# The beginning of a two-layer decoder trunk written out: the first norm's weights on the transposed side, loads in turns, casts and low halves by k-tile

## The chip, the cores and the metric

One of the cores of a Trainium2 chip runs the whole program, one launch for both layers. The metric is the device time of one execution in microseconds (us), lower is better. The engines are called as in the profile: PE (TensorE, the matrix engine), PEld (its loads of stationary tiles), DVE (VectorE), ACT (ScalarE), POOL (GpSimd) and SP (SyncE, which here only issues DMAs).

## What is computed

The reference takes x of 256 x 1024 numbers in float32 and applies two layers, each of three sub-layers with a norm before and behind it:

```python
def rms_norm(x, g):
    y = x * lax.rsqrt(jnp.mean(x * x, axis=-1, keepdims=True) + EPS)
    return y * g

def swiglu(h, wi, wo):
    gate, up = jnp.split(h @ wi, 2, axis=-1)
    return (jax.nn.silu(gate) * up) @ wo

for l in range(2):
    x = x + 0.5 * rms_norm(swiglu(rms_norm(x, ffn1_pre_g[l]), ffn1_wi[l], ffn1_wo[l]), ffn1_post_g[l])
    x = x + rms_norm(hybrid_mixer(rms_norm(x, mix_pre_g[l]), ...), mix_post_g[l])
    x = x + 0.5 * rms_norm(swiglu(rms_norm(x, ffn2_pre_g[l]), ffn2_wi[l], ffn2_wo[l]), ffn2_post_g[l])
```

The change touches the very first rms_norm, of x with ffn1_pre_g[0], and the first two pieces of ffn1_wi[0], which is 1024 x 5632. The mixer (a gated, a windowed and a stick-breaking branch) is not touched.

## The kernel before

The 256 rows of x lie in two tiles of 128 rows, called tt = 0 and 1 (x0 and x1 in the trace). Products in float32 precision are made of three matmuls of a narrower type (fp32r): each operand is split into a high half (a cast) and a low half (what the cast left), and `mm3` (L391 to L395) adds high by high, low by high and high by low (L392, L393, L394).

**Weights.** The host packs all weights in 212 units of 1 MB, each 128 x 2048 numbers, in the order of use. `loader` (L161) brings a unit into one of two buffers called raw, by SP's queue, in an order kept by `load` (L113); `stream` lets the next unit go out when the buffer two back has been split. `splitter` (L213) casts each half unit to hi on ACT (L231) and subtracts it to lo on DVE (L232), into rings of eight halves. raw2 can thus be loaded only when the low halves of unit 0 are done, raw3 when those of unit 1 are, and so on by turns of two.

**Activations.** `prenorm` (L344) makes a norm: two Squares with their sums on ACT (L350), the power −1/2 on POOL (`rstd_of`, L315), the product xn of x, that factor rs and the weights gain on DVE (L360), then `to_T` (L335): per half, four transposes on PE into a tile tr (L339), and `hilo` (L330), which writes hh on ACT (L332) and hl on DVE (L333), each 128 x 512. The weights of a norm come by `gain` (L279) as a tile of 128 x 1024, a broadcast load of 512 KB.

**The first feed-forward.** A chunk (`chunk512`, L397) is 512 columns of wi, 256 of the gate and 256 of the other, for one row tile: 8 k-tiles, so 24 matmuls, over two units. Its product goes through Silu on ACT (L451) and a product on DVE (L452) into sg, and two transposes bring sg to gT, which the second matrix product (accumulators acc) uses. Four chunks with tt = 0 and 1 in turn come first; from the fifth on pairs of chunks are made with seven products instead of eight (`pair7`), which want sums of the activations: `sums` (L487) makes tiles sA on DVE (L491, L502, L506, L507, L513) and splits them (ACT L496, DVE L497). The quads of weights for this (wa, wb, wf) are in part loaded with accumulating DMAs.

**What sets the order.** The code is run by a model clock: each group of matmuls lets `ck` advance by the PE time it is given, and coroutines (the splitter, norms, sums, transposes of sg) say by `yield` how many us later they go on. So an instruction's place in its engine's row depends on this clock. Ahead of it all stands the beginning: x0, gain0, raw0 in two halves, x1 and raw1 are issued on SP one behind the other; `prenorm` of tt = 0 starts at 4.0, of tt = 1 at 10.0, the splitter at 7.0 of the model's time; ten warming matmuls of 128 x 128 on an identity run ahead on PE.

Of the kernel before, what the change touches and what calls it, by code (L numbers as in the profile page):

```python
# [9 lines left out]
F32 = mybir.dt.float32  # L10
# [64 lines left out]


@with_exitstack
def trunk(ctx, tc, x, wpk, gains, lnp, wst, bst, consts, out, depth=DEPTH):
    nc = tc.nc
    V, S, G, T = nc.vector, nc.scalar, nc.gpsimd, nc.tensor  # L80
    ck = Clock()
# [17 lines left out]
    def tr_tile(n):  # L99
        return ptr.tile([P, 512], F32, tag="tr", name=nm(n))  # L100
# [12 lines left out]
    def load(dst, src):  # L113

        i = nc.sync.dma_start(dst, src)
        if lastdma[0] is not None:
            tc.add_manual_dep(i.ins, lastdma[0].ins.name, NOSYNC, reason="load order")
        lastdma[0] = i
# [41 lines left out]

    def loader():  # L161

        ring = []

        def stream(key, u, first=False):
            while len(ring) >= 2 and ring[-2] not in done:
                yield
            ring.append(key)
            t = rp.tile([P, 2048], F32, tag="raw", name=f"raw{u}", bufs=2)
            raw[key] = [t[:, c] for c in WQ]  # L170
            for c in WQ if first else (slice(0, 2048),):
                load(t[:, c], wpk[u][:, c])

        def load_b(k):
            f = k.ffn
            i = "b" + str(k.par)
            if i not in f:
                f[i] = [sp.tile([P, 1024], F32, tag="q4", name=nm("wb"), bufs=9),
                        sp.tile([P, 1024], F32, tag="shl" if k.par else "q4", name=nm("wb"), bufs=1 if k.par else 9)]
            k.b = f[i]  # L180
            for q, c in enumerate(WQ):
                load(k.b[q], wpk[k.u12][:, c])
            for q, c in enumerate(WQ):
                nc.gpsimd.dma_start(k.b[q], wpk[k.u22][:, c], accum_op=ALU.add)

        for n, (kind, k) in enumerate(plan):
            if n + 4 < NI and plan[n + 4][0] == "B11" and not plan[n + 4][1].prev:
                load_b(plan[n + 4][1])
            if kind == "w":
                yield from stream(n, k, n == 0)  # L190
            elif kind == "B11":
                while k.prev and not k.prev.t1:
                    yield
                f = k.ffn
                if "a" not in f:
                    f["a"] = [sp.tile([P, 1024], F32, tag="q4", name=nm("wa"), bufs=9) for _ in WQ]
                raw[n] = f["a"]
                for q, c in enumerate(WQ):
                    load(f["a"][q], wpk[k.u11][:, c])
            elif kind in ("B21", "B22"):  # L200
                yield from stream(n, k.u21 if kind == "B21" else k.u22)
                if kind == "B21" and k.next:
                    load_b(k.next)
            yield
# [3 lines left out]
    def ready(n, kind, k):  # L208
        if kind[0] == "T":
            raw[n] = k.b if kind == "T3" else k.ffn["a" if kind == "T1" else "f"]  # L210
        return n in raw

    def splitter():  # L213
        for n, (kind, k) in enumerate(plan):
            while not ready(n, kind, k):
                next(ld)
            halves[n] = []
            for q in range(2):
                gate = place.get(n)
                while st_["free"] <= 0 if gate is None else not gate.on:  # L220
                    yield 0.2
                    gate = place.get(n)
                if gate is not None:
                    h = sp.tile([P, 1024], F32R, tag="q4", name=f"hi{n}_{q}", bufs=9)
                    lo = sp.tile([P, 1024], F32R, tag="q4", name=f"lo{n}_{q}", bufs=9)
                else:
                    st_["free"] -= 1
                    h = rp.tile([P, 1024], F32R, tag="hi", name=f"hi{n}_{q}", bufs=RING)
                    lo = rp.tile([P, 1024], F32R, tag="lo", name=f"lo{n}_{q}", bufs=RING)
                r = raw[n][q]  # L230
                S.copy(h, r)  # L231
                V.tensor_sub(lo, r, f32(h))  # L232
                halves[n].append((h, lo))
                yield 1.2
            if kind == "B11":
                f = k.ffn
                if "f" not in f:
                    f["f"] = [sp.tile([P, 1024], F32, tag="xn", name=nm("wf"), bufs=2) for _ in WQ]
                for q, c in enumerate(WQ):
                    V.tensor_add(f["f"][q], f["a"][q], k.b[q])  # L240
                    nc.gpsimd.dma_start(f["a"][q], wpk[k.u12][:, c], accum_op=ALU.add)
                    yield 0.6
            elif kind == "B21":
                for q in range(2):
                    V.tensor_add(k.ffn["f"][q], k.ffn["f"][q], raw[n][q])
                    yield 0.6
            elif kind == "T1":
                k.t1 = True
            done.add(n)
            for _ in range(3):  # L250
                next(ld, None)
# [31 lines left out]
            gl[i] = t  # L283
        return gl.get(i)

    load(xs[0], x[0:P, :])
    gain(0)
    next(ld)
    load(xs[1], x[P:SEQ, :])
    next(ld)  # L290

    mB_ = cp.tile([P, 1152], BF16, tag="mB", name="mB")
    mB = [mB_[:, 768:1152], mB_[:, 0:768]]
# [50 lines left out]
    def prenorm(tt, gi, flag, st=None):  # L344

        xn = sp.tile([P, DM], F32, tag="xn", name=nm("xn"), bufs=2)
        st = sp.tile([P, 2], F32, tag="ss", name=nm("ss"), bufs=4)
        for i, h in enumerate(HF):
            with tc.high_priority(offset=HOT):
                q = S.activation(xn[:, h], xs[tt][:, h], AF.Square, scale=DM ** -0.5, accum_out=st[:, i:i + 1])  # L350
                if gi == 0 and tt == 1:
                    tc.add_manual_dep(q.ins, lasthi[0].ins.name, NOSYNC, reason="first tile first")
            if i == 0:
                yield 0.6
        r = rstd_of(st[:, 0:1], st[:, 1:2])
        yield 1.7
        gn = gain(gi)
        with tc.high_priority(offset=HOT):
            for h in HF:
                V.scalar_tensor_tensor(xn[:, h], xs[tt][:, h], r, gn[:, h], op0=ALU.mult, op1=ALU.mult)  # L360
        yield 1.0
        for i, h in enumerate(HF):
            to_T(xn[:, h], tt, 4 * i, 4, hh, hl)
            yield 0.7
        flag.on = True

    def post_half(acc, yn, st, i, gi, mul):

# [555 lines left out]
            finish(tt, gi + 1, acc, us[3], hh, hl, 6, 6, KD, tt == 1, 1.0, nxt)  # L924


    ck.start(splitter(), 7.0)
    for tt in range(NT):
        hready[tt] = Flag()
        co = prenorm(tt, 0, hready[tt])  # L930
        ck.start(co, 4.0 + 6 * tt)
    warm = tr_tile("warm")
    for i in range(10):
        T.matmul(warm[:, 0:P], ident, ident, start=True, stop=True)
    for l in range(depth):
        b = 6 * l
        ffn(b, b + 2, l == 0)
# [101 lines left out]
```

## Time and profile before

| | us |
|---|---|
| median of 3 runs | 1259.87 |
| lowest and highest | 1258.27 and 1259.88 |
| the profiled execution | 1260.91 |
| its span in the trace | 1259.2 |
| PE busy | 1240.5 |
| DVE busy | 949.3 |
| ACT busy | 729.5 |
| POOL busy | 75.5 |

The profiled execution takes 1.7 us more than the span that the trace shows. Busy time says how long an engine executed; PE's busy time counts overlapping matmuls once. In a timeline a row is a run of like instructions: start, length from the first start to the last end, engine, line, operation, what it writes and reads, their count, and in brackets how long the engine stood idle before and what ended that. A row for two instructions is shorter than twice one, since the second begins before the first's end. In the chain of waits a DMA's row goes from issue to landing.

### The profile page before, as it was taken

The numbers are of one execution on the slowest core, as the hardware profiler recorded it, in microseconds if no ns is written. First come the engines' busy times: TensorE is split into PE (matmuls) and PEld (weight loads), VectorE is DVE, ScalarE is ACT, GpSimd is POOL, SyncE is SP. The second block draws the span as 40 slices with busy tenths as digits, with TensorE's granted clock in tenths as the row PEclk, the third lists the DMA queues.
The fourth block names the chain that finished last, engine by engine and source line by source line (L and its number), as shares of the span: only waits on it lengthen the run. The fifth ranks groups of instructions, "written<-read, shape, count | busy, mean of one in ns | idle before, by whom it ended". The sixth has DMA issues, their size and how long they took to land.

```text
span 1259.2 us, 16367 instructions
## 1 busy us (share of the span) xinstructions
PE 1240.5 (99%) x6284; PEld 1029.3 (82%) x6284; DVE 949.3 (75%) x1185; ACT 729.5 (58%) x996; POOL 75.5 (6%) x129
## 2 busy tenths in 40 slices
PE   8999999999999999999999999999999999999997
PEld 6777878998778878888878888789977788888886
DVE  5889977645765877899768899865467668689983
ACT  5566656435656465666645666654366655557652
POOL 0001001000000010010011010010000000110000
PEclk8999999999999999999999999999999999999999
DMA  7899555554435557885668785744543455687851
GB/s 251 279 316 264 172 201 194 188 212 166 136 134 178 192 167 271 261 270 167 239 207 260 252 258 185 236 175 161 210 181 119 149 173 200 213 240 250 250 195 65
DMA packets 45294, 259.41 MB, mean 206 GB/s; under 512 B 5280, under 2 KB 5408, under 8 KB 21280
## 3 DMA queue, kind: packets, MB, share of 16 engines
q1 hardware_dynamic: 38304, 233.20, 52.0%
q0 software_dynamic: 6912, 25.17, 10.5%
q8 instruction: 49, 0.80, 0.3%
q14 instruction: 29, 0.24, 0.1%
HBM read 257.30 MB, written 1.05 MB: 205 GB/s over the span
## 4 chain that ended last, share of the span: by engine, by line
PE 82%; DMA 6%; DVE 6%; ACT 3%; issue 1%; POOL 1%; SPq 0%; DVEq 0%; POOLq 0%; ACTq 0%
PE mm L392 15%; PE mm L394 15%; PE mm L393 15%; DMA raw<-wpk 5%; PE acc L394 5%; PE acc L393 5%; PE acc L392 5%; DVE lo L232 3%; PE qk L393 3%; PE qk L394 3%; PE qk L392 3%; PE tr L339 2%; ACT hi L231 2%; PE pj L394 1%; PE pj L392 1%; PE pj L393 1%
## 5 line engine op out<-in xcount | busy, mean ns | idle before, releaser
L232 DVE TENSOR_TENSOR lo<-raw,hi 128x1024 fp32r<-128x1024 f32 x376 | 451.8, 1220 | 153.2 <-ACT hi L231 148.1
L231 ACT CAST hi<-raw 128x1024 fp32r<-128x1024 f32 x376 | 387.2, 1050 | 259.4 <-DMA raw<-wpk 78.6
L392 PE MATMUL mm<-hi,hh 128*128 128x512 f32 x784 | 314.0, 401 | 1.7 <-ACT hh L332 1.7
L394 PE MATMUL mm<-hi,hl 128*128 128x512 f32 x784 | 307.3, 392 | 0.2 <-DVE hl L333 0.2
L393 PE MATMUL mm<-lo,hh 128*128 128x512 f32 x784 | 306.8, 391 | 0.0
L392 PEld LDWEIGHTS mm<-hi,hh 128*128 128x128 f32 x784 | 147.9, 189 | 33.3 <-issue 2.7
L394 PEld LDWEIGHTS mm<-hi,hl 128*128 128x128 f32 x784 | 147.7, 188 | 32.7 <-DVE hl L333 0.9
L393 PEld LDWEIGHTS mm<-lo,hh 128*128 128x128 f32 x784 | 148.1, 189 | 27.9
L392 PE MATMUL acc<-hi,gT 128*128 128x512 f32 x352 | 139.3, 396 | 0.2 <-ACT gT L332 0.2
L394 PE MATMUL acc<-hi,gT 128*128 128x512 f32 x352 | 137.6, 391 | 0.3 <-DVE gT L333 0.3
L393 PE MATMUL acc<-lo,gT 128*128 128x512 f32 x352 | 137.7, 391 | 0.0
L392 PE MATMUL qk<-hh,hi 128*128 128x256 f32 x320 | 91.2, 285 | 0.0
L394 PE MATMUL qk<-hh,lo 128*128 128x256 f32 x320 | 90.5, 283 | 0.0
L393 PE MATMUL qk<-hl,hi 128*128 128x256 f32 x320 | 90.5, 283 | 0.0
L392 PE MATMUL mm<-hi,sA 128*128 128x512 f32 x192 | 77.2, 402 | 0.8 <-DVE sg L479 0.8
L394 PEld LDWEIGHTS acc<-hi,gT 128*128 128x128 f32 x352 | 66.1, 188 | 14.3 <-DVE gT L333 0.8
L392 PEld LDWEIGHTS acc<-hi,gT 128*128 128x128 f32 x352 | 66.1, 188 | 13.5 <-ACT gT L332 0.7
L393 PEld LDWEIGHTS acc<-lo,gT 128*128 128x128 f32 x352 | 66.2, 188 | 13.0
L394 PE MATMUL mm<-hi,sA 128*128 128x512 f32 x192 | 75.1, 391 | 0.0
L393 PE MATMUL mm<-lo,sA 128*128 128x512 f32 x192 | 74.9, 390 | 0.0
L332 ACT CAST gT<-tr 128x256 fp32r<-128x256 f32 x88 | 32.5, 369 | 63.6 <-PE tr L339 63.5
L393 PEld LDWEIGHTS qk<-hl,hi 128*128 128x128 f32 x320 | 61.4, 192 | 0.1
(170 smaller groups left out, 1724.2 us busy)
## 6 DMA issues: line engine op xcount, KB each, us to landing
raw<-wpk SPq DMA_DIRECT2D x187, 1024.0 KB, 4.9
wb<-wpk SPq DMA_DIRECT2D x24, 512.0 KB, 7.0
wb<-wpk POOLq DMA_DIRECT2D x24, 512.0 KB, 9.2
wa<-wpk SPq DMA_DIRECT2D x24, 512.0 KB, 6.0
wa<-wpk POOLq DMA_DIRECT2D x24, 512.0 KB, 9.5
gain<-gains SPq DMA_DIRECT2D x12, 512.0 KB, 7.7
x<-x SPq DMA_DIRECT2D x2, 512.0 KB, 5.6
raw<-wpk SPq DMA_DIRECT2D x2, 512.0 KB, 6.5
```

Of the source, the lines that this page charges most:

```text
L231: S.copy(h, r)
L232: V.tensor_sub(lo, r, f32(h))
L332: lasthi[0] = S.copy(h_out, src)
L339: T.transpose(tr[:, k * P:(k + 1) * P], src[:, k * P:(k + 1) * P], ident)
L392: T.matmul(o, ah, bh, start=first, stop=False, skip_group_check=go_on)
L393: T.matmul(o, ah, bl, start=False, stop=False, skip_group_check=go_on)
L394: T.matmul(o, al, bh, start=False, stop=stop, skip_group_check=go_on)
```

## The change

The first norm and the first two units are no longer made by `prenorm`, `loader` and `splitter`, but by a new function `begin`, which says the order of ACT and of DVE row by row:

- The norm's weights come as gk, a tile of 128 x 8 (4 KB, one column per k-tile) by a DMA that ACT issues. The load of gain0 is gone. xn is x times rs alone, and the weights are applied behind the transposes: hh is an ACT activation (Copy) with a column of gk as scale, hl one DVE operation with that column, each per k-tile (128 x 128), so eight and eight for each row tile where there were two and two.
- x0 comes in two halves. The Square of its second half is on DVE.
- Loads go out in turns: x0, raw0's first half; raw0's second half behind the first Square; x1 behind the first cast; then raw1 in two halves. `loader` and `splitter` begin at unit 2.
- Unit 0 is cast by k-tile (128 x 512), and its low halves stand between the hl of the first group. x1's Squares stand behind the first cast of unit 1.
- Eleven warming matmuls run ahead, and two more between the two groups of transposes of x0.
- The splitter starts at 0.0 of the model's clock behind this, and the groups of tt = 1 are a coroutine `second` that starts with a wait of 3.0.

Its core; the tile sizes, the clock and all that follows the first feed-forward's code are as before:

```diff
@@ loader @@
-        ring = []
-
-        def stream(key, u, first=False):
+        ring = [0, 1]
...
-            for c in WQ if first else (slice(0, 2048),):
-                load(t[:, c], wpk[u][:, c])
+            load(t, wpk[u])
...
+            if n < 2:
+                continue
...
-    load(xs[0], x[0:P, :])
-    gain(0)
-    next(ld)
-    load(xs[1], x[P:SEQ, :])
-    next(ld)
...
-                if gi == 0 and tt == 1:
-                    tc.add_manual_dep(q.ins, lasthi[0].ins.name, NOSYNC, reason="first tile first")
...
+    gk = cp.tile([P, KD], F32, tag="gk", name="gk")
+    first = {}
+    def order(eng, i):
+        if eng in first:
+            tc.add_manual_dep(i.ins, first[eng].ins.name, NOSYNC, reason="order of the beginning")
+        first[eng] = i
+        return i
+    def scaled(tt, st):
+        xn = sp.tile([P, DM], F32, tag="xn", name=nm("xn"), bufs=2)
+        r = rstd_of(st[:, 0:1], st[:, 1:2])
+        for h in HF:
+            order("V", V.tensor_scalar(xn[:, h], xs[tt][:, h], r, None, op0=ALU.mult))
+        return xn
+    def group(xn, tt, i, lows):
+        tr = tr_tile("tr")
+        for k in range(4):
+            T.transpose(tr[:, k * P:(k + 1) * P], xn[:, (4 * i + k) * P:(4 * i + k + 1) * P], ident)
+        ck.pe(0.43)
+        for k in range(4):
+            kk = 4 * i + k
+            order("S", S.activation(hh[:, tt, kk, :], tr[:, k * P:(k + 1) * P], AF.Copy, scale=gk[:, kk:kk + 1]))
+        for k in range(4):
+            kk = 4 * i + k
+            lows[k]()
+            order("V", V.scalar_tensor_tensor(hl[:, tt, kk, :], tr[:, k * P:(k + 1) * P], gk[:, kk:kk + 1],
+                                              f32(hh[:, tt, kk, :]), op0=ALU.mult, op1=ALU.subtract))
+    def begin():
+        warm = sc_tile("warm")
+        def warmup(n):
+            for _ in range(n):
+                T.matmul(warm[:, 0:P], ident, ident, start=True, stop=True)
+        def after(i, j):
+            tc.add_manual_dep(i.ins, j.ins.name, mybir.DependencyInfo(
+                mybir.DependencyClass.Sync, mybir.DependencyReason.SCHED_ONLY), reason="loads in turn")
+        warmup(11)
+        nc.scalar.dma_start(gk, g0)
+        for h in HF:
+            load(xs[0][:, h], x[0:P, h])
+        rt = [rp.tile([P, 2048], F32, tag="raw", name=f"raw{u}", bufs=2) for u in range(2)]
+        ht, lt = [], []
+        for u in range(2):
+            for q in range(2):
+                ht.append(rp.tile([P, 1024], F32R, tag="hi", name=f"hi{u}_{q}", bufs=RING))
+                lt.append(rp.tile([P, 1024], F32R, tag="lo", name=f"lo{u}_{q}", bufs=RING))
+        st_["free"] -= 4
+        load(rt[0][:, WQ[0]], wpk[0][:, WQ[0]])
+        st = sp.tile([P, 2], F32, tag="ss", name=nm("ss"), bufs=4)
+        sq = sp.tile([P, DM], F32, tag="xn", name=nm("sq"), bufs=2)
+        i0 = order("S", S.activation(sq[:, HF[0]], xs[0][:, HF[0]], AF.Square, scale=DM ** -0.5,
+                                     accum_out=st[:, 0:1]))
+        order("V", V.scalar_tensor_tensor(sq[:, HF[1]], xs[0][:, HF[1]], 1.0 / DM, xs[0][:, HF[1]], op0=ALU.mult,
+                                          op1=ALU.mult, accum_out=st[:, 1:2]))
+        load(rt[0][:, WQ[1]], wpk[0][:, WQ[1]])
+        after(lastdma[0], i0)
+        def hi(n, k):
+            c = slice(512 * (k % 2), 512 * (k % 2) + 512)
+            return order("S", S.copy(ht[2 * n + k // 2][:, c], rt[n][:, 512 * k:512 * k + 512]))
+        def low(n, k):
+            c = slice(512 * (k % 2), 512 * (k % 2) + 512)
+            j = 2 * n + k // 2
+            order("V", V.tensor_sub(lt[j][:, c], rt[n][:, 512 * k:512 * k + 512], f32(ht[j][:, c])))
+        i1 = hi(0, 0)
+        hi(0, 1)
+        load(xs[1], x[P:SEQ, :])
+        after(lastdma[0], i1)
+        for q in range(2):
+            load(rt[1][:, WQ[q]], wpk[1][:, WQ[q]])
+        xn = scaled(0, st)
+        def lo2(k):
+            if k == 2:
+                hi(0, 2)
+                hi(0, 3)
+            low(0, k)
+        group(xn, 0, 0, [lambda k=k: lo2(k) for k in range(4)])
+        warmup(2)
+        group(xn, 0, 1, [lambda: None] * 4)
+        for q in range(2):
+            halves.setdefault(0, []).append((ht[q], lt[q]))
+        hready[0].on = True
+        for q in range(2):
+            j = 2 + q
+            order("S", S.copy(ht[j], rt[1][:, WQ[q]]))
+            if q == 0:
+                st = sp.tile([P, 2], F32, tag="ss", name=nm("ss"), bufs=4)
+                sq = sp.tile([P, DM], F32, tag="xn", name=nm("sq"), bufs=2)
+                for i, h in enumerate(HF):
+                    order("S", S.activation(sq[:, h], xs[1][:, h], AF.Square, scale=DM ** -0.5,
+                                            accum_out=st[:, i:i + 1]))
+            order("V", V.tensor_sub(lt[j], rt[1][:, WQ[q]], f32(ht[j])))
+            halves.setdefault(1, []).append((ht[j], lt[j]))
+            if q == 0:
+                xn = scaled(1, st)
+        for n in range(2):
+            done.add(n)
+            raw[n] = True
+        def second():
+            yield 3.0
+            for i in range(2):
+                group(xn, 1, i, [lambda: None] * 4)
+                yield 0.7
+            hready[1].on = True
+        ck.start(second(), 0.0)
...
-    ck.start(splitter(), 7.0)
     for tt in range(NT):
         hready[tt] = Flag()
-        co = prenorm(tt, 0, hready[tt])
-        ck.start(co, 4.0 + 6 * tt)
-    warm = tr_tile("warm")
-    for i in range(10):
-        T.matmul(warm[:, 0:P], ident, ident, start=True, stop=True)
+    begin()
+    ck.start(splitter(), 0.0)
...
+        "g0": np.ascontiguousarray(gains[0].reshape(KD, P).T),
```

On DVE, in the place of the first row tile's end and the second's beginning, the row before was this (xn, then low halves of unit 1, hl of tt = 1, low halves of units 2 and 3):

```order
L360 SCALAR_TENSOR_TENSOR xn_8_148<-x1_81,rs_10_159,gain0_83 128x512 x2
L232 TENSOR_TENSOR lo1_0_141<-raw1_89,hi1_0_140 128x1024
L232 TENSOR_TENSOR lo1_1_155<-raw1_89,hi1_1_154 128x1024
L333 TENSOR_TENSOR hl_95<-tr_11_189,hh_94 128x512
L333 TENSOR_TENSOR hl_95<-tr_13_206,hh_94 128x512
L232 TENSOR_TENSOR lo2_0_171<-raw2_138,hi2_0_170 128x1024
L232 TENSOR_TENSOR lo2_1_183<-raw2_138,hi2_1_182 128x1024
L452 TENSOR_TENSOR sg_14_213<-mm_7_144,sg_14_213 128x256
L232 TENSOR_TENSOR lo3_0_202<-raw3_168,hi3_0_201 128x1024
```

and it is now this, where gk is the small tile of weights:

```order
L468 TENSOR_TENSOR lo1_0_110<-raw1_104,hi1_0_109 128x1024
L378 TENSOR_SCALAR xn_10_170<-x1_81,rs_11_171 128x512 x2
L468 TENSOR_TENSOR lo1_1_112<-raw1_104,hi1_1_111 128x1024
L235 TENSOR_TENSOR lo2_0_185<-raw2_182,hi2_0_184 128x1024
L235 TENSOR_TENSOR lo2_1_195<-raw2_182,hi2_1_194 128x1024
L393 SCALAR_TENSOR_TENSOR hl_86<-tr_13_215,gk_87,hh_85 128x128 x4
L393 SCALAR_TENSOR_TENSOR hl_86<-tr_14_238,gk_87,hh_85 128x128 x4
L235 TENSOR_TENSOR lo3_0_209<-raw3_204,hi3_0_208 128x1024
L235 TENSOR_TENSOR lo3_1_232<-raw3_204,hi3_1_231 128x1024
```

The eight small hl of tt = 1 (L393) now stand behind the low halves of unit 2, and one low half of unit 1 stands ahead of xn.

On ACT, in the same place, the row before:

```order
L231 CAST hi1_0_140<-raw1_89 128x1024
L231 CAST hi1_1_154<-raw1_89 128x1024
L231 CAST hi2_0_170<-raw2_138 128x1024
L332 CAST hh_94<-tr_11_189 128x512
L332 CAST hh_94<-tr_13_206 128x512
L231 CAST hi2_1_182<-raw2_138 128x1024
L451 ACT_TABLE_LOAD
L451 ACTIVATE sg_14_213<-mm_7_144 128x256
```

and now:

```order
L461 CAST hi1_0_109<-raw1_104 128x1024
L466 ACTIVATE sq_9_166,ss_8_165<-x1_81 128x512 x2
L461 CAST hi1_1_111<-raw1_104 128x1024
L389 ACTIVATE hh_85<-tr_13_215,gk_87 128x128 x2
L234 CAST hi2_0_184<-raw2_182 128x1024
L234 CAST hi2_1_194<-raw2_182 128x1024
L389 ACTIVATE hh_85<-tr_13_215,gk_87 128x128 x2
L389 ACTIVATE hh_85<-tr_14_238,gk_87 128x128 x4
L569 ACT_TABLE_LOAD
```

x1's Squares stand between the two casts of unit 1, and six of the eight small hh behind both casts of unit 2.

On DVE again, from unit 7's low halves to the silu product sg that PE's transposes await, the row before:

```order
L232 TENSOR_TENSOR lo7_0_353<-raw7_289,hi7_0_352 128x1024
L232 TENSOR_TENSOR lo7_1_372<-raw7_289,hi7_1_371 128x1024
L507 TENSOR_TENSOR sA_34_394<-sA_30_369,sA_34_394 128x512
L491 TENSOR_TENSOR sA_41_446<-hh_94,hl_95 128x512
L513 TENSOR_TENSOR sA_41_446<-sA_41_446,sA_34_394 128x512
L232 TENSOR_TENSOR lo8_0_413<-raw8_350,hi8_0_412 128x1024
L232 TENSOR_TENSOR lo8_1_429<-raw8_350,hi8_1_428 128x1024
L497 TENSOR_TENSOR sA_33_391<-sA_30_369,sA_33_391 128x512
L497 TENSOR_TENSOR sA_38_421<-sA_34_394,sA_38_421 128x512
L497 TENSOR_TENSOR sA_40_443<-sA_29_367,sA_40_443 128x512
L497 TENSOR_TENSOR sA_42_461<-sA_41_446,sA_42_461 128x512
L452 TENSOR_TENSOR sg_45_469<-mm_39_424,sg_45_469 128x256
```

and now, where five more rows follow up to that product (four of the operation L615 that L497 was, then sg_47):

```order
L235 TENSOR_TENSOR lo7_0_388<-raw7_324,hi7_0_387 128x1024
L609 TENSOR_TENSOR sA_32_404<-hh_85,hl_86 128x512
L331 TENSOR_TENSOR gT_24_346<-tr_39_436,gT_24_346 128x256
L235 TENSOR_TENSOR lo7_1_407<-raw7_324,hi7_1_406 128x1024
L620 TENSOR_TENSOR sA_32_404<-sA_31_402,sA_32_404 128x512
L609 TENSOR_TENSOR sA_36_429<-hh_85,hl_86 128x512
L609 TENSOR_TENSOR sA_43_481<-hh_85,hl_86 128x512
L624 TENSOR_TENSOR sA_31_402<-sA_36_429,sA_31_402 128x512
L235 TENSOR_TENSOR lo8_0_448<-raw8_385,hi8_0_447 128x1024
L625 TENSOR_TENSOR sA_36_429<-sA_32_404,sA_36_429 128x512
L235 TENSOR_TENSOR lo8_1_464<-raw8_385,hi8_1_463 128x1024
L631 TENSOR_TENSOR sA_43_481<-sA_43_481,sA_36_429 128x512
```

Of the sums sA, two of the operation L609 (L491 before), one L620 (L502) and one L624 (L506), and one gT product, now stand behind the first low half of unit 7; they stood ahead of it.

On PE the transposes of that product were in this place before:

```order
L394 MATMUL mm_44_465<-hi6_1_340,hl_95 128x512
L392 MATMUL acc_26_359<-hi7_0_352,gT_22_311 128x512
L393 MATMUL acc_26_359<-lo7_0_353,gT_22_311 128x512
L339 MATMUL tr_46_488<-ident_73,sg_45_469 128x128 x2
L394 MATMUL acc_26_359<-hi7_0_352,gT_22_311 128x512
L392 MATMUL acc_27_360<-hi7_0_352,gT_22_311 128x512
```

and are now here:

```order
L512 MATMUL mm_46_500<-hi6_0_360,hl_86 128x512
L510 MATMUL mm_46_500<-hi6_1_375,hh_85 128x512
L511 MATMUL mm_46_500<-lo6_1_376,hh_85 128x512
L337 MATMUL tr_48_523<-ident_73,sg_47_504 128x128 x2
L512 MATMUL mm_46_500<-hi6_1_375,hl_86 128x512
L510 MATMUL mm_46_500<-hi6_1_375,hh_85 128x512
L511 MATMUL mm_46_500<-lo6_1_376,hh_85 128x512
L512 MATMUL mm_46_500<-hi6_1_375,hl_86 128x512
```

They stand six matmuls further forward: two of the accumulating ones (acc) were ahead of them, and now four of the last chunk's (mm) come behind them. In the rows of all engines past some 60 us, and of POOL from the start, names' numbers aside, before and after read alike.

## Rows read from the trace of the kernel before

**Rows 1.** The page's first part: engine, busy us, share of the span, instructions.

```profile
PE 1240.5 (99%) x6284; PEld 1029.3 (82%) x6284; DVE 949.3 (75%) x1185; ACT 729.5 (58%) x996; POOL 75.5 (6%) x129
```

**Rows 2.** Waits of PE over the span: us in total, times, longest.

```profile
PE tr L339 <- DVE sg L452: 3.0, 5, 1.5
...
PE mm L392 <- DVE sg L479: 0.8, 2, 0.6
```

**Rows 3.** Timeline of PE, 0 to 62 us.

```profile
7.62 1.38 PE L339 MATMUL tr<-ident,xn 128*128 128x128 f32 x8 [1.57 <-DVE xn L360]
10.66 0.79 PE L392 MATMUL mm<-hi,hh 128*128 128x512 f32 x1 [1.66 <-ACT hh L332]
...
20.71 0.39 PE L394 MATMUL mm<-hi,hl 128*128 128x512 f32 x1
...
56.16 0.44 PE L339 MATMUL tr<-ident,sg 128*128 128x128 f32 x2 [1.54 <-DVE sg L452]
```

**Rows 4.** Chain of waits, 0 to 62 us: start, length, what.

```profile
14.11 0.43 PE mm L392
...
20.42 0.23 PE mm L392
...
24.51 0.22 PE tr L339 x2
...
35.69 9.96 DMA raw<-wpk
```

**Rows 5.** Timeline of ACT, 0 to 62 us.

```profile
4.39 0.63 ACT L350 ACTIVATE xn<-x 128x512 f32<-128x512 f32 x1 [2.32 <-DMA x<-x]
...
5.54 0.19 ACT L350 ACTIVATION_READ_ACCUMULATOR xn<-x 128x1 f32 x1
...
19.87 1.28 ACT L451 ACT_TABLE_LOAD   x1
...
45.72 2.00 ACT L231 CAST hi<-raw 128x1024 fp32r<-128x1024 f32 x2 [4.12 <-DMA raw<-wpk]
```

**Rows 6.** Timeline of DVE, 0 to 62 us.

```profile
6.81 1.41 DVE L360 SCALAR_TENSOR_TENSOR xn<-x,rs,gain 128x512 f32<-128x512 f32 x2 [6.81 <-POOL rs L325]
8.88 2.50 DVE L232 TENSOR_TENSOR lo<-raw,hi 128x1024 fp32r<-128x1024 f32 x2 [0.66 <-ACT hi L231]
...
26.11 1.23 DVE L232 TENSOR_TENSOR lo<-raw,hi 128x1024 fp32r<-128x1024 f32 x1 [0.52 <-ACT hi L231]
...
38.37 1.28 DVE L491 TENSOR_TENSOR sA<-hh,hl 128x512 f32<-128x512 f32 x2
...
42.44 0.42 DVE L333 TENSOR_TENSOR gT<-tr,gT 128x256 fp32r<-128x256 f32 x1
...
46.80 2.36 DVE L232 TENSOR_TENSOR lo<-raw,hi 128x1024 fp32r<-128x1024 f32 x2 [3.35 <-ACT hi L231]
```

**Rows 7.** Windows: stretch, length, busy PE, PEld, DVE, ACT, POOL, PEclk, DMA, GB/s.

```profile
10.00:20.00 10.00, 9.18 (x31) 6.95 (x32) 7.77 (x11) 7.42 (x14) 0.88 (x2) 0.66 0.68 238
```

**Rows 8.** Groups of one form: busy us, mean ns, idle before, releaser.

```profile
L332 ACT CAST hh<-tr 128x512 fp32r<-128x512 f32 x32 | 18.6, 586 | 24.2 <-PE tr L339 24.1
...
L713 ACT ACTIVATE eC<-eC 128x768 f32<-128x768 f32 x16 | 13.5, 846 | 0.4
...
L713 ACT ACTIVATE pB<-pB,stB 128x768 f32<-128x768 f32 x8 | 7.5, 935 | 5.3 <-POOL stB L733 5.3
...
L656 DVE SCALAR_TENSOR_TENSOR u<-sv,bs,u 128x128 f32<-128x128 f32 x16 | 4.5, 343 | 0.0
...
L644 DVE TENSOR_SCALAR v<-v,bn,rs 128x512 f32<-128x512 f32 x4 | 2.2, 547 | 6.0 <-POOL rs L325 6.0
```

**Rows 9.** Loads of tile raw, 0 to 62 us.

```profile
DMA to landing us min/median/max: 4.8/6.1/10.0
```

**Rows 10.** Loads of tile x, 0 to 62 us.

```profile
DMA to landing us min/median/max: 3.6/5.6/7.7
```

**Rows 11.** The page's part on DMA issues: count, KB each, us to landing.

```profile
bs<-bst SPq DMA_DIRECT2D x2, 2.0 KB, 6.3
```

More of the change, by code (lines that the diff above doesn't have):

```diff
@@ L77, in trunk @@
 @with_exitstack
-def trunk(ctx, tc, x, wpk, gains, lnp, wst, bst, consts, out, depth=DEPTH):
+def trunk(ctx, tc, x, wpk, gains, g0, lnp, wst, bst, consts, out, depth=DEPTH):
     nc = tc.nc
@@ L161, in loader, with stream @@
     def loader():
-        ring = []
-        def stream(key, u, first=False):
+        ring = [0, 1]
+        def stream(key, u):
             while len(ring) >= 2 and ring[-2] not in done:
@@ L189, in loader @@
             if kind == "w":
-                yield from stream(n, k, n == 0)
+                yield from stream(n, k)
             elif kind == "B11":
@@ L214, in splitter @@
         for n, (kind, k) in enumerate(plan):
+            if n < 2:
+                continue
             while not ready(n, kind, k):
```

## The prediction

> **What bounds the kernel now.** I read the page first: TensorE (PE) is busy for 99% of the span [rows 1], so a change to the first microseconds pays only as far as a wait of PE goes away for good. The list of PE's waits [rows 2] and its timeline [rows 3] are read next. Two waits lie in the beginning that is rewritten: 1.57 us for xn before the transposes at 7.62, and 1.66 us for hh before the first matmul at 10.66. But the longest of the five waits for sg, 1.54 us, lies at 56.16, behind the beginning. The chain of waits [rows 4] says what holds that place: a raw tile issued at 35.69 that needs 9.96 us to land. ACT casts it at 45.72 [rows 5], VectorE (DVE) starts its low halves at 46.80 [rows 6], and only with what it has in its order behind them comes the silu product sg that PE transposes at 56.16. A lead won at the front is worth nothing if PE only waits longer at 56.16, so this place decides. The clock is the third thing to see: 0.66 in the slice from 10 to 20 us [rows 7], with a 512-column matmul each 0.43 us at 14.11 and each 0.23 us at 20.42 [rows 4]: half level (1.2 GHz) first, then full.
>
> The sum is made on the profiled execution, 1260.91 us (span 1259.2 and 1.7 around it). That is 1.04 over the median 1259.87; the difference found is set on the median. 0.2%, 2.5 us, is about what a measurement can tell from no change.
>
> **The front: 2.0 to 2.5 us won.** Before, ACT squares both halves of x0, from 4.39 to 5.73 [rows 5]; Pool's rs takes 1.08 from there to xn at 6.81 [rows 6]. After, DVE takes the second half (an operation with the shape of the old xn, of which two take 1.41 [rows 6]: 0.75 for one), so rs is there at 4.35 + 0.75 + 1.08 = 6.2, with hand-offs 6.3. xn is then a TENSOR_SCALAR, 0.55 [rows 8]: first half 6.85. Four transposes (two in 0.22 [rows 4]) end at 7.3. hh now takes four activations with a tile as scale. No row has 128 columns on ACT. A cast of 1024 columns takes 1.05 (two in 2.00, 0.95 apart [rows 5]) and one of 512 takes 0.586 [rows 8], so by the columns one of 128 takes 0.24; a tile as operand adds 0.935 − 0.846 = 0.09 (L713 with and without [rows 8]). The bounds are 0.24 and the 0.586 of four times the columns; I take 0.35, near the lower because the size is, with 0.26 from one to the next. The four run under other work: PE has two warming matmuls and four more transposes (0.43 at full level, 0.85 at half) ahead of the first matmul, which starts at 8.2 to 8.6, not 10.66. gk must be there by 7.3. Its nearest row, the load of 2 KB into a tile of 128 x 4, takes 6.3 [rows 11]; issued at 0.8 it lands at 7.1. So hidden, by a thin cover.
> By page "ScalarE: Activation LUTs" of the Trainium skill (section "What ACT_TABLE_LOAD costs"), an activation costs 186 ns and 0.833 ns a column, and each pointer operand 93 ns more: 0.386 us here, which speaks against replacing one cast by four. By it the steps of this sum that run through hh would be 0.26 us later in all, and the forecast 1261.5; L713's difference agrees with the 93 ns, but no row shows so short an activation.
>
> **Unit 0's buffer and raw2.** The low halves, 2.50 from 8.88 before [rows 6] and so done at 11.38, are now four of 512 columns between four small hl. Raw0's second half, issued at 5.0 behind the first Square, lands 3.6 later (the shortest x [rows 10]); two casts, then the last low half at 10.75 to 10.95. raw2 goes out 0.4 to 0.6 earlier.
>
> **Unit 1 and tile 1: the holding back costs what the front won.** raw0's first half lands at 5.6 to 6.6 (x's 4.35 and 1.2 to 2.2 us for half a megabyte more: 1.2 is the difference between the shortest raw, 4.8, and the shortest x, 3.6 [rows 9, 10]). x1 goes out only after its first cast (0.59), so at 6.2 to 7.2, lands 3.6 later at 9.85 to 10.85, and raw1's half follows 1.2 behind. hi1_0 (1.05) ends at 12.1 to 13.1, x1's squares stand behind it in ACT's order (1.34, as for x0), then rs 1.08, xn 0.55, four transposes, two of the hh, with 0.2 of hand-offs: hi2_0 on ACT starts at T2 = 16.3 to 17.3. If PE is at half level, 18 matmuls of 0.43 ahead of the transposes make that up to 18.2. I take 17.2.
>
> **The second chunk.** DVE's order now has lo2_0 and lo2_1 ahead of tile 1's eight hl; before, hl came first. With hi2_0 and hi2_1 0.95 apart, 1.22 for each low half and 0.34 for the first hl (L656 [rows 8]), the first matmul that needs an hl of tile 1 starts at T2 + 3.8 = 20.1 to 22.0. The like matmul of before, third of its chunk, stands at 20.71 [rows 3]. So of the lead of 2.0 to 2.5 us what is left here is between +0.6 and −1.3.
>
> **The chain of loads.** Behind the hl stand lo3_0 and lo3_1: from T2, two casts, six hh (0.35, then 0.26 apart), the table load (1.28 [rows 5]), sg (256 columns, between the cast's 0.24 and 0.59 of 128 and 512: 0.38), two casts and one low half give, with 0.2 of hand-offs, T2 + 8.65 = 24.95 to 26.85. Before, that was 26.11 + 1.23 = 27.34 [rows 6]. It frees the buffer for raw5, whose lo5 frees that for raw7. So raw7 is issued 2.4 to 0.5 earlier; I take 1.5, with the same 9.96 us on the way, since the accumulating loads beside it move along.
>
> **From raw7 to sg: 4.1 us lost.** From 46.80 to PE's transposes at 56.16 it took 9.36 before. In DVE's new order, four sums (L609 twice, L620, L624) and one gT product that stood ahead of lo7_0 stand behind it. DVE did them before at 36 to 43, while raw7 was on its way (of the sums two at 38.37, gT at 42.44 [rows 6]); now they are queued between raw7 and sg. That is 4 × 0.60 (two in 1.28, 0.68 for one) + 0.34 for gT (0.42 less what overlaps the next) = 2.74. On PE sg's transposes stand six matmuls further forward, which must still be run behind the wait: 6 × 0.23 = 1.36. So the place at 56.16 is later by 2.74 + 1.36 − 1.5 = 2.6 (1.7 to 3.6). PE itself arrives earlier and only waits longer.
>
> **Behind 56 us.** All engines' orders are those of before past some 60 us. Later waits can take the delay up: sg 1.5 (3.0 less the 1.54) and 0.8 [rows 2], 2.3 at most. Those are waits for a DVE that is late with it, so I take 1.3. The result is +1.3 us (−1.1 to +3.6): **1261.2 us**, 1262.2 for the profiled execution.
> The gain(0) load of 512 KB that goes away, the eleventh warming matmul and the earlier start of the splitter are costed at nothing: the first lies beside loads that are awaited, and shows in the landing times taken above; PE stands idle anyway where the second runs; without that cover each is under 1.3 us.
>
> **Rivals.** *Half level to the end of the second chunk (slower).* PE runs earlier here while data are short; if it stays at half level past T2, T2 is 18.2, the chain of loads ends at 26.85 and raw7 gains only 0.5 or nothing. It decides when the first chunk's 18 matmuls ahead of tile 1's transposes run at 0.43. The place at 56 is then 3.6 to 4.6 later, and with 0.1 to 1.3 taken up behind it: 1262.2 to 1264.4, say 1263.4. For it: before, the clock fell after PE's two waits; against it: these waits are now shorter. 0.2.
> *raw7 lands sooner (faster).* The 9.96 us are long beside the median of 6.1 [rows 9]. If its new place among the transfers lets it land in 7.4 or less, the place at 56 doesn't move back, 2.6 − 2.6 = 0, and at the shortest landing of 4.8 it moves forward by 5.2 − 2.6 = 2.6, to which an earlier DVE adds up to 0.5 of the later waits: 1256.8 to 1259.9. For it: raw7 is issued before the accumulating loads have all started. Against: these were beside it before also. 0.25.
> *The held loads or gk come late (nothing won at the front).* If gk lands 2.5 us past 7.3, the first matmul stands at 10.66 again, and T2, which hangs on x1, doesn't move: the sum is the forecast's, +0 to +1: 1260.9 to 1262.2. It is within the forecast's bounds. 0.05.
>
> **How the numbers follow.** Forecast 0.5 (its own bounds 1258.8 to 1263.5), slower rival 0.2, faster 0.25, held loads 0.05. The range that leaves out 2 in 10, 0.13 of it below, is 1257.4 to 1264.0. Faster by over 2.5 us, under 1257.35, takes the faster rival's short landing: half of it, 0.12, and 0.03 for a front that gains more than I see: 0.15. Slower, over 1262.4, is most of the slower rival (0.15) and the forecast's upper end (0.08): 0.23. The rest, 0.62, is no change.
>
> **What would show it.** PE's timeline: first matmul at 8.2 to 8.6; the third matmul of the second chunk at 20 to 22; a wait of about 4 to 5 us for sg near 56 to 59 (1.54 before), with sg's transposes at 57.4. DVE's timeline: lo7_0 at 44.4 to 46.3 and some 11.6 us from it to sg. ACT: hi2_0 at 16.3 to 17.3, small activations of 0.35. The forecast is wrong if the wait for sg does not grow (raw7 landed in under 8), if DVE's low halves ran ahead of where T2 puts them, or if PE keeps the front's lead through 60 us: then the time is below 1259.

## The result: 12 us slower

The changed kernel takes 1271.89 us (median of 5 runs, 1268.78 to 1273.17), the kernel before 1259.87 (1258.27 to 1260.71): a ratio of 1.0084, 95% interval 1.0065 to 1.0103 (the quotient of the two medians is 1.0095). The range went to 1264.0, so the prediction was wrong. The profiled execution of the changed kernel is the median one: 1271.89, span 1270.2, 11.0 over the 1259.2 of before. PE's busy time alone grew by 11.6, though it runs only six instructions more (three warming matmuls, each recorded as two). The page's first part, as in [rows 1]:

```profile
PE 1252.1 (99%) x6290; PEld 1029.2 (81%) x6290; DVE 953.3 (75%) x1201; ACT 731.7 (58%) x1008; POOL 75.3 (6%) x129
```

PE's timeline in the beginning, which answers to [rows 3]:

```profile
8.29 0.50 PE L510 MATMUL mm<-hi,hh 128*128 128x512 f32 x1
...
14.01 0.49 PE L510 MATMUL mm<-hi,hh 128*128 128x512 f32 x1 [1.49 <-ACT hi L461]
...
22.72 0.50 PE L512 MATMUL mm<-hi,hl 128*128 128x512 f32 x1 [1.68 <-DVE hl L393]
...
59.58 0.44 PE L337 MATMUL tr<-ident,sg 128*128 128x128 f32 x2 [3.48 <-DVE sg L570]
...
62.34 0.63 PE L512 MATMUL acc<-hi,gT 128*128 128x512 f32 x1
```

The first matmul comes 2.4 us earlier than before, then PE waits for unit 1 (1.49 us ahead of 14.01), for the first hl of tile 1 (1.68 ahead of 22.72) and for sg (3.48 ahead of 59.58). The matmul at 62.34 is the one that stood right behind sg's transposes, at 56.36: the beginning has left PE 6.0 us behind. Up to there the story is of the kind forecast, if larger. Behind it the forecast had nothing to say, and there it went wrong. The waits of PE behind 62 us, first of before and then of after, are the next view (us in total, times, longest):

```profile
PE tr L339 <- DVE xn L360: 1.7, 3, 0.8
PE tr L339 <- DVE sg L452: 1.5, 4, 0.6
PE mm L392 <- DVE sg L479: 0.8, 2, 0.6
PE trB L745 <- DVE pB L738: 0.5, 2, 0.3
...
```

```profile
PE tr L337 <- DVE sg L570: 0.6, 2, 0.3
PE acc L510 <- ACT gT L330: 0.3, 1, 0.3
PE acc L512 <- DVE gT L331: 0.3, 1, 0.3
```

PE waits less than before there (1.2 us in all, 5.5 before), and yet it falls back by another 5 us up to the end. So its matmuls themselves must be slower. A stretch in the first mixer without any wait, in which one row of matmuls runs from the second to the 75th, shows it at the same granted clock of 1.00. Of before:

```profile
386.99 0.40 PE L393 MATMUL mm<-lo,hh 128*128 128x512 f32 x1
...
403.60 0.39 PE L394 MATMUL mm<-hi,hl 128*128 128x512 f32 x1
```

And the same matmuls of after:

```profile
392.83 0.39 PE L511 MATMUL mm<-lo,hh 128*128 128x512 f32 x1
...
409.86 0.39 PE L512 MATMUL mm<-hi,hl 128*128 128x512 f32 x1
```

73 steps take 16.61 us before and 17.03 after: 227.5 ns a matmul, and 233.3. Sorted by operands over the whole trace, those in which hh or hl stands as an operand of 128 columns while 512 columns stream (the three kinds of mm and of wo, 3 × 784 and 3 × 64) have become slower, by 5.5 ns on the mean; those with gT or sA in its place have not (acc: 227.5 in both). 2544 × 5.5 ns is 14 us. Two smaller groups, qk and mmv, have become faster; they come below.

### The profile page after: what moved, and what is told of

Read it like the earlier page. It is cut to its first block, busy times and chain, and to the rows that moved or that the text cites. A ratio compares the mean times of both kernels' runs of the same rounds, so it can differ in the third digit from the quotient of the medians.

```text
span 1270.2 us, 16413 instructions
## 1 busy us (share of the span) xinstructions
PE 1252.1 (99%) x6290; PEld 1029.2 (81%) x6290; DVE 953.3 (75%) x1201; ACT 731.7 (58%) x1008; POOL 75.3 (6%) x129
## 4 chain that ended last, share of the span: by engine, by line
PE 92%; DMA 3%; DVE 2%; ACT 1%; issue 0%; POOL 0%; SPq 0%; DVEq 0%; POOLq 0%; ACTq 0%
PE mm L510 17%; PE mm L512 17%; PE mm L511 17%; PE acc L512 6%; PE acc L511 6%; PE acc L510 6%; PE qk L512 3%; PE qk L511 3%; PE qk L510 3%; DMA raw<-wpk 3%; PE tr L337 2%; PE pj L510 1%; PE pj L511 1%; PE pj L512 1%; DVE lo L235 1%; PE wo L510 1%
## 5 line engine op out<-in xcount | busy, mean ns | idle before, releaser
L510 PE MATMUL mm<-hi,hh 128*128 128x512 f32 x784 | 317.8, 405 | 1.6 <-ACT hi L461 1.5
L512 PE MATMUL mm<-hi,hl 128*128 128x512 f32 x784 | 311.3, 397 | 2.1 <-DVE hl L393 2.1
L511 PE MATMUL mm<-lo,hh 128*128 128x512 f32 x784 | 311.3, 397 | 0.8 <-DVE lo L468 0.8
L235 DVE TENSOR_TENSOR lo<-wf,hi 128x1024 fp32r<-128x1024 f32 x48 | 58.5, 1221 | 3.6 <-ACT hi L234 2.9
```

The costliest lines, as they stand in the source:

```text
L510: T.matmul(o, ah, bh, start=first, stop=False, skip_group_check=go_on)
L511: T.matmul(o, ah, bl, start=False, stop=False, skip_group_check=go_on)
L512: T.matmul(o, al, bh, start=False, stop=stop, skip_group_check=go_on)
```

## The experiments

**What the order of instructions doesn't show.** gk is a tile of 32 bytes a partition of SBUF, the memory from which the engines read their operands, and it is taken from the first pool, behind hh and hl. All that is placed behind it moves up by 32 bytes: raw, hi, lo, gT, sA. hh and hl stay. So in mm hi and lo, which stream through PE, have changed place against hh and hl, which stand in it (the 128 columns that PEld loads ahead), and not against gT and sA, which stand in it in other matmuls. Theory A is that this distance is what costs. Its rival, theory B, is that the beginning has shifted all engines' work against each other, so that something collides later.

```diff
 # e1: gk of 64 bytes, of which half is used
-    gk = cp.tile([P, KD], F32, tag="gk", name="gk")
+    gk = cp.tile([P, 2 * KD], F32, tag="gk", name="gk")[:, 0:KD]
 # e2: gk ahead of hh and hl, so that these move too
+    gk = cp.tile([P, KD], F32, tag="gk", name="gk")
     hh = cp.tile([P, NT, KD, P], F32R, tag="hh", name="hh")
     hl = cp.tile([P, NT, KD, P], F32R, tag="hl", name="hl")
...
-    gk = cp.tile([P, KD], F32, tag="gk", name="gk")
 # e3 (32 bytes), p64 (64), g1 (96): the kernel before with an idle tile behind hl; e4: 32 ahead of hh
     hl = cp.tile([P, NT, KD, P], F32R, tag="hl", name="hl")
+    pad = cp.tile([P, KD], F32, tag="pad", name="pad")
+    G.memset(pad, 0.0)
 # g4: the kernel before with mB (2304 bytes) allocated behind hl instead of ahead of hh
```

> The changed kernel with gk's tile widened from 32 to 64 bytes a partition (a view of 8 of 16 columns), nothing else: all tiles behind it in SBUF lie 32 bytes further on, so hi, lo, gT and sA start again at 32 over a multiple of 64 bytes, as hh and hl do, and as they did before the change. Theory A (address): the mm matmuls with hh and hl as one operand, 233 ns in the changed kernel and 227.7 before, go back to under 229, and the time falls from 1271.9 to the beginning's own cost, 1262 to 1265. Theory B (the slow matmuls come from how the other engines' work now falls beside them, or from the chip): same order of work, so 1270 to 1273 and 233 ns stay.

> The changed kernel with gk's tile (32 bytes) placed ahead of hh and hl instead of behind: now hh, hl, hi, lo, gT, sA all start at a multiple of 64 bytes. Theory A in the form 'both operands must have the same place in 64 bytes': 227 to 229 ns, time as the one with 64 bytes, 1262 to 1265. Theory A in the form 'moving operands at a multiple of 64 bytes are slow': 233 ns for all, also for acc and sA, and 1275 or more. Theory B: 1270 to 1273.

> The kernel before with an idle tile of 32 bytes a partition between hl and the raw buffers (one small memset on POOL more), nothing of the beginning changed: hi, lo, gT, sA at a multiple of 64 bytes, hh and hl 32 bytes over one, as in the changed kernel. Theory A: the 2,540 or so matmuls with hh and hl go from 227.7 to 233 ns, 13.5 us in all, of which 2 to 4 are taken up by waits that vanish: 1269 to 1272. Theory B: 1260.

> The kernel before with the idle tile of 32 bytes ahead of hh: hh, hl, hi, lo, gT, sA all at a multiple of 64 bytes. Theory A, same place in 64 bytes: 1258 to 1261, no change, 227 to 229 ns. Theory A, moving operands at a multiple of 64 are slow: all mm and acc at 233 and 1275 or more. Theory B: 1260.

> The kernel before with an idle tile of 64 bytes between hl and the raw buffers: hi and lo lie 64 bytes off hh's place in 128 bytes, but at the same place in 64. If only the place in 64 bytes counts: 227.7 ns for mm, 120 for qk, 1259.5. If that in 128 bytes counts too, as e1's rows say: mm with hh and hl at 229.2, qk at 116, so +2540 times 1.5 ns and -960 times 4.5 ns, and 1258.5 to 1259.5.

> The kernel before with an idle tile of 96 bytes between hl and the raw buffers: hi and lo lie 96 bytes from hh's place in 128 (0 before, 32 in the changed kernel, 64 in p64). If an odd multiple of 32 is what costs, whichever way: mm with hh and hl at 233, qk near 118, 1267 to 1271. If only exactly 32 on costs: 228 to 230 and 1258 to 1261.

> The kernel before with the mask tile mB (2304 bytes) placed behind hl instead of ahead of hh: hi and lo lie 256 bytes from hh's place in 512. If the place in 128 bytes is what counts: mm 227.7 and qk 120 to 122 ns, 1259.5. If a larger period counts, mm or qk change by over 1 ns.

The stretch of 73 steps was read in each trace. The distance is that of hi and lo from hh in bytes, less whole multiples of 128, worked out from the sizes of the tiles. The ratio is to executions of the kernel before that were taken beside each run, not to the first row.

| kernel | distance | 73 matmuls, us | one, ns | median, us | ratio to before, 95% |
|---|---|---|---|---|---|
| before | 0 | 16.61 | 227.5 | 1259.87 | |
| changed | 32 | 17.03 | 233.3 | 1271.89 | 1.0084 (1.0065 to 1.0103) |
| e1, changed, gk of 64 bytes | 64 | 16.72 | 229.0 | 1259.96 | 1.0012 (0.9999 to 1.0024) |
| e2, changed, gk ahead of hh | 0 | 16.61 | 227.5 | 1261.59 | 1.0019 (1.0007 to 1.0031) |
| e3, before, 32 idle bytes | 32 | 17.03 | 233.3 | 1268.17 | 1.0070 (1.0053 to 1.0086) |
| e4, before, 32 ahead of hh | 0 | 16.61 | 227.5 | 1259.49 | 1.0005 (0.9992 to 1.0017) |
| p64, before, 64 idle bytes | 64 | 16.72 | 229.0 | 1258.33 | 0.9990 (0.9981 to 0.9999) |
| g1, before, 96 idle bytes | 96 | 17.03 | 233.3 | 1269.03 | 1.0074 (1.0061 to 1.0088) |
| g4, before, mB moved | 0 (256 in 512) | 16.61 | 227.5 | 1258.91 | 0.9990 (0.9981 to 0.9999) |

The two rows of e3, where nothing of the beginning is changed, and the two of e2, where all of it is:

```profile
387.34 0.39 PE L395 MATMUL mm<-lo,hh 128*128 128x512 f32 x1
...
404.37 0.39 PE L396 MATMUL mm<-hi,hl 128*128 128x512 f32 x1
```

```profile
389.15 0.40 PE L511 MATMUL mm<-lo,hh 128*128 128x512 f32 x1
...
405.76 0.39 PE L512 MATMUL mm<-hi,hl 128*128 128x512 f32 x1
```

Theory B falls with both: 32 idle bytes in the old kernel bring 8.7 us of the loss, and the whole new beginning without the shift brings 2.4 (3.9 at most) of 12. It isn't where hi and lo start by themselves either: in e4 and e2 they start at the multiple of 64 bytes at which they start in the changed kernel, and are fast, and hh starts there too. In this stretch distances of 32 and 96 cost the same 5.8 ns, 64 costs 1.5, 0 and 256 nothing.

One thing doesn't fit the distance alone. In g1 the matmuls with sA take 230.5 ns (mean of the steps without a wait), in the kernel before 228.0, though sA, hi and lo have moved there together. Something beside the distance counts in g1, the place that the two tiles share or another cause; no run parts them. With 576 such matmuls it is 1.4 us at most of g1's loss of 9.

The products that make q and k for the attention (qk, where hh and hl stream, 256 columns, and hi and lo stand) go the other way. 161 steps of qk take 19.39 us before (239.24 to 258.63 in PE's timeline), 19.14 in the changed kernel (244.73 to 263.87) and 18.34 in e1, whose rows are:

```profile
242.88 0.37 PE L510 MATMUL qk<-hh,hi 128*128 128x256 f32 x1
...
261.22 0.28 PE L512 MATMUL qk<-hh,lo 128*128 128x256 f32 x1
```

It isn't the exchange of roles that turns the sign. In mmv, which makes a part of the attention's values, hh and hl stand as in mm, only 256 columns of hi and lo stream, and it gains too. First and last of its 48 matmuls in the first mixer, before and then after:

```profile
269.66 0.28 PE L392 MATMUL mmv<-hi,hh 128*128 128x256 f32 x1
...
275.29 0.28 PE L394 MATMUL mmv<-hi,hl 128*128 128x256 f32 x1
```

```profile
275.18 0.28 PE L510 MATMUL mmv<-hi,hh 128*128 128x256 f32 x1
...
280.67 0.28 PE L512 MATMUL mmv<-hi,hl 128*128 128x256 f32 x1
```

The 47 steps take 5.63 us before, 5.49 after (distance 32), 5.33 in e1 (64) and 5.64 in g1 (96). These gains fit that e1, with mm at 229.0, isn't slower than e2, and that e1 and e3 came out below what was expected of them (1262 to 1265, and 1269 to 1272), where no gain was counted. p64's ratio of 0.999 is no proof of a gain by it: g4, in which mm and qk take what they took before, has the same ratio.

**What the beginning itself costs.** e2 is the changed kernel without the address effect, so the forecast is to be held against it: 1.0019, or +2.4 us (0.9 to 3.9), where +1.3 was forecast. Theory C says that this is the place of the sums behind raw7, theory D that it is the loads held back. On e2's base:

```diff
 # f1, f3: the splitter later, so that three of the four sums and the gT stand ahead of unit 7's low halves
-    ck.start(splitter(), 0.0)
+    ck.start(splitter(), 4.0)
 # f2, f3: no load held; g3 takes only the second line out
-        after(lastdma[0], i0)
...
-        after(lastdma[0], i1)
 # g2: f2 with gk of 64 bytes behind hl
```

> The changed kernel with gk ahead of hh (so that the address effect is gone: e2, 1261.6), and the splitter started at 4.0 of the model's clock instead of 0.0. That puts tile 1's first four hl ahead of unit 2's low halves and three of the four sums and the gT product back ahead of unit 7's low halves, as in the kernel before. Theory C (what the beginning still costs is the place of these sums): the wait for sg near 56 to 59 falls from 2.2 us to under 1, the half-level stretch behind it goes, and the time falls to 1257 to 1259.5. Theory D (it is the loads held back, by which unit 1, and with it raw5 and raw7, come late): the time stays at 1260.5 to 1262.

> As e2, but no load is held back: raw0's second half and x1 go out when SP comes to them. Order of all engines as in e2. Theory C: 1261 to 1262, since the sums still stand behind raw7, although unit 1's cast comes at 11 to 12 instead of 12.9 to 13.6. Theory D: raw7 is issued 1.5 to 2 us earlier and the time falls to 1259 to 1260.

> Both: splitter at 4.0 and no load held back. Theory C: as with the splitter at 4.0 alone, 1257 to 1259.5. Theory D: as without held loads alone, 1259 to 1260. If both count, 1256 to 1258, under the kernel before.

> As e2 (1261.6), but only raw0's second half is held back (behind the first Square), x1 no longer behind the first cast. Theory D as the prediction put it, x1's hold makes unit 1 late: hi1_0 starts at 11 to 12.3 instead of 13.8 in e2, and the time is that without any hold, 1259 to 1260. If it is raw0's second half: 1261 to 1262.

> The beginning without held loads (f2, 1259.5), with gk of 64 bytes behind hl, so that hi and lo lie 64 bytes from hh's place as in p64 (1258.3, 0.8 to 1.3 us under the kernel before). If the two are independent: 1258 to 1259, a ratio of 0.999 to the kernel before. No change: 1259.5.

| kernel | held loads | splitter | hi1_0 starts | raw7 (f1, f3: raw8) issued, on the way | wait for sg, transposes at | median, us | ratio to before, 95% |
|---|---|---|---|---|---|---|---|
| e2 | two | 0.0 | 13.84 | 37.17, 8.53 | 2.24, 58.83 | 1261.59 | 1.0019 (1.0007 to 1.0031) |
| f1 | two | 4.0 | 13.06 | 43.36, 9.50 | 4.34, 59.20 | 1261.69 | 1.0020 (1.0010 to 1.0030) |
| g3 | raw0's second half | 0.0 | 12.93 | 35.88, 9.38 | 3.10, 58.40 | 1261.29 | 1.0015 (1.0000 to 1.0029) |
| f2 | none | 0.0 | 11.91 | 34.83, 8.38 | 2.02, 56.35 | 1259.53 | 1.0003 (0.9994 to 1.0012) |
| f3 | none | 4.0 | 11.81 | 42.60, 8.86 | 3.81, 57.80 | 1259.83 | 1.0001 (0.9990 to 1.0011) |
| g2 | none | 0.0 | 12.03 | 34.93, 8.72 | 2.29, 56.78 | 1258.50 | 0.9989 (0.9978 to 1.0000) |

The runs speak for theory D. Without held loads unit 1's first cast starts at 11.81 to 12.03 (f2, f3, g2), with both held at 12.92 to 13.84 (the changed kernel, e1, e2, f1). From e2 to f2 raw7 is issued 2.3 us earlier, sg's transposes come 2.5 earlier, and the time is that of the kernel before. It is a difference of 2 us, and the intervals of e2 and f2 overlap, but f1 and f3, which differ by the held loads alone, show the same 1.9 us. With x1 free but raw0's second half still held (g3), the cast starts at 12.93, no earlier than in the changed kernel with both held, and the interval of its time parts it neither from e2 nor from f2; which of the two holds costs more stays open. ACT's rows of the first cast of unit 1, of e2 and of f2:

```profile
13.84 1.04 ACT L461 CAST hi<-raw 128x1024 fp32r<-128x1024 f32 x1 [2.85 <-DMA raw<-wpk]
```

```profile
11.91 1.09 ACT L459 CAST hi<-raw 128x1024 fp32r<-128x1024 f32 x1
```

Theory C falls. In f1 the sums stand ahead of unit 7's low halves, and yet PE's transposes of sg don't come earlier, because unit 8's load now ends last. DVE's timeline of f1:

```profile
48.51 2.36 DVE L235 TENSOR_TENSOR lo<-raw,hi 128x1024 fp32r<-128x1024 f32 x2 [4.25 <-ACT hi L234]
...
54.04 2.36 DVE L235 TENSOR_TENSOR lo<-raw,hi 128x1024 fp32r<-128x1024 f32 x2 [1.24 <-ACT hi L234]
```

Between raw7 and sg it takes 10.7 us (48.51 to 59.20), where the changed kernel takes 12.0 (47.60 to 59.58). DVE has time to spare for 1.24 of it, waiting for the cast of raw8, which was issued at 43.36 and took 9.50. So the order I found in the trace as a cost was real, but another wait stood a microsecond behind it. PE's clock belongs to the account too. Behind its wait of 4.34 us f1 runs nine steps at 0.43 (60.11 to 63.95). Where all are at full level again (the matmul at 65.80 of before), e2 is 5.1 us late (70.94), f1 4.8 (70.60) and f2 1.1 (66.93). So f1 has next to nothing of its earlier sums, and f2 leads e2 by 4.0: 2.5 by sg, and the rest by a stretch of half level that it doesn't have (granted clock 1.00 from 60 to 65 us, 0.78 in e2). g2 puts the two findings together; at 0.9989 (0.9978 to 1.0000) it is at best level with the kernel before, so no version here beats that kernel clearly.

## Why the prediction was wrong, by its steps

**The step that failed is "Behind 56 us".** It said that all engines' orders past some 60 us are those of before, counted the later waits that could take up a delay, and let every later matmul take as long as before. The orders were as said. But the change part by part had costed gk by its DMA and its reads, and not by its 32 bytes: no term asked what lies behind it in SBUF. In the traces, the kinds of matmul from the one at 62.34 on add up to +5.0 us: 8.9 more for mm with hh and hl, waits between them included, 1.5 less for qk, 1.6 less for mm with sA, which waits less, and smaller pieces. Of the slack that PE had (5.5 us of waits behind 62 us) 4.3 went into it. So the term was put at nothing without a reason; e3 measures it without the beginning: +8.7 us (1268.17 less 1259.48, the median of before beside it).

That the beginning by itself, +2.4 in e2, came near the +1.3 is in part luck. At the first matmul that both orders have behind sg's transposes (56.36 before, 61.88 in e2) e2 is 5.5 us late, where 2.6 was forecast; its span is 2.0 longer, so 3.5 was taken up behind it, where 1.3 was forecast. Two bounds don't follow from their terms: 1.7 less 2.3 is −0.6 and not −1.1, and with raw7 gaining 0.5 or nothing the slower rival's place is 3.6 to 4.1 later, not 4.6. Neither bears on the miss.

**The front** came as forecast: first matmul at 8.29 (8.2 to 8.6). An activation of 128 columns took 0.377 (median of 16), not 0.35. This is the place where the prediction drew on "ScalarE: Activation LUTs" of the Trainium skill (section "What ACT_TABLE_LOAD costs"), whose 0.386 was the nearer. gk landed after 3.0 us, not 6.3, so the thin cover was thick:

```profile
L389 ACT ACTIVATE hh<-tr,gk x16: 354/377/407, 7.9 to 22.1; 128x128 fp32r<-128x128 f32 x16
...
DMA to landing us min/median/max: 3.0/3.0/3.0
```

**Unit 1 and tile 1** were too early in the forecast. ACT and the chain of waits of the changed kernel, which answer to [rows 4, 5]:

```profile
6.83 1.14 ACT L432 CAST hi<-raw 128x512 fp32r<-128x512 f32 x2 [2.49 <-DMA raw<-wpk]
...
12.92 1.04 ACT L461 CAST hi<-raw 128x1024 fp32r<-128x1024 f32 x1 [1.84 <-DMA raw<-wpk]
...
18.96 1.99 ACT L234 CAST hi<-raw 128x1024 fp32r<-128x1024 f32 x2
...
46.52 2.00 ACT L234 CAST hi<-raw 128x1024 fp32r<-128x1024 f32 x2 [5.61 <-DMA raw<-wpk]
```

```profile
7.84 5.05 DMA raw<-wpk
...
27.56 6.15 DMA raw<-wpk
...
37.26 9.19 DMA raw<-wpk
```

raw1's first half was issued at 7.84 and needed 5.05, so it landed at 12.9 and not at 11.05 to 12.05. Two terms were too short. raw0's first half landed at 6.81, not at 5.6 to 6.6, so x1 went out at 7.47; x1 then took 3.65, as forecast (3.6), but raw1's half landed 1.8 behind it and not 1.2. hi2_0 came at 18.96 (17.2 taken, 18.2 at most), the third matmul of the second chunk at 22.72 (20.1 to 22.0). raw5 was issued at 27.56, not earlier than before, and took 6.15. So raw7 went out 1.6 us later than before, not 1.5 earlier; only its shorter way, 9.19 for 9.96, gave 0.8 of it back. The 11.6 us from lo7_0 to the transposes were 12.0.

**The half level of PE's clock.** The forecast had it in the first chunk only. It shows again right behind the long wait for sg. The windows from 10 to 20 us (0.66 before, [rows 7]) and from 60 to 65 (1.00 before) of the changed kernel:

```profile
10.00:20.00 10.00, 7.75 (x26) 5.33 (x26) 6.25 (x13) 5.84 (x15) 0.87 (x2) 0.83 0.71 240
60.00:65.00 5.00, 5.00 (x17) 3.95 (x16) 5.00 (x7) 2.27 (x4) 0.00 (x0) 0.67 0.59 210
```

From 59.77 to 63.20 the matmuls stand 0.43 apart, eight of them before the level rises: 8 × 0.2 = 1.6 us. Six of them are those that now stand behind the transposes: 6 × 0.43 = 2.6, where 1.36 was forecast, and with the 3.4 of the transposes (59.58 less 56.16) this makes the 6.0 of lateness. In f2, where the clock stays at 1.00 from 10 to 30 us, the half-speed stretch of before is gone, and the time is that of before all the same: PE then waits for lo, hl and sg instead.

**The rivals.** None of the three named the mechanism. The slower one's sign hardly came: of the first chunk's 18 matmuls ahead of tile 1's transposes four ran at 0.43. The half level that cost time lies behind the wait for sg, and the result of 1271.9 lies 7.5 us past this rival's end. The faster one's condition failed: raw7 took 9.19, not 7.4. Of the third, gk was early, and the held loads didn't delay the front.

## What to carry to other kernels

A new small tile moves every tile that is allocated behind it: compare the addresses of the two operands of the most frequent matmul before and after an edit, as one compares the orders. Where both addresses moved together the time stayed, where they moved apart by 32 bytes 0.7% of the whole kernel was gone (e3), so put small tiles behind the large ones, or where they leave that distance as it was. And before a load is held back so that another lands first, follow what waits for the held one: here it fed a chain of buffers whose end, 45 us later, was PE's longest wait.

## What the runs showed of the hardware

A matmul of 512 columns in fp32r takes 227.5 ns where the standing and the streaming tile lie at the same place in 128 bytes of SBUF, 229.0 at 64 bytes' distance and 233.3 at 32 and 96; qk's steps of 256 columns take 120.4 ns at distance 0 (19.39 us in 161), 118.9 at 32, 113.9 at 64 and 117.9 at 96 (18.98 us in 161, in g1). mmv's 47 steps of 256 columns take 5.63, 5.49, 5.33 and 5.64 us at these distances. The Trainium skill, page "SBUF — State Buffer", section "Operand start alignment", asks only that an operand start at a multiple of its element size, and calls this a rule about legality and not speed; all the tiles here keep it, and the traces show a cost in time beside it. Why matmuls of 256 columns gain from the distance at which those of 512 lose, and whether the loads of the standing tiles or the streams are what is held up, no run here parts.
